# The blocks beyond an expert's slots: from a branch after every expert to one late place, and 96 slots for the largest expert

## The chip, the cores and the metric

One core of one Trainium2 chip runs the whole program in one launch. The metric is the device time of one execution in microseconds; of several executions the median is given. The kernel is fp32 throughout the part that the change touches. A row of the profile names an instruction by its line in kernel.py, its engine and the tiles that it writes and reads: PE is TensorE (PEld its weight loads), DVE is VectorE, ACT is ScalarE, POOL is GpSimd, SP is SyncE, which here only issues transfers. PEq, SPq and so on are the sequencers of those engines.

## What is computed

One layer of an encoder block on 256 tokens of width 1024: a layer norm, a gated attention mixer, a second layer norm, and then a mixture of 32 experts, of which each token takes its 4 best. The change touches the experts alone. Per expert the reference does, on the tokens that chose it,

```
hb = xb @ w_exp_in[e] + b_exp_in[e]          # 1024 -> 2048
g  = min(hb[:, :1024], 7);  u = clip(hb[:, 1024:], -7, 7)
y  = (g * sigmoid(1.702 * g) * (u + 1)) @ w_exp_out[e] + b_exp_out[e]   # 1024 -> 1024
```

and each token's four results are summed with its softmax weights. A last layer norm of `alpha * h + f` gives the output. How many tokens an expert gets is known only when the program runs; the 32 counts sum to 1024.

## The kernel before

**Places and slots.** All 32 experts are worked through, one after another, in 32 places (`for pos in range(NE)`, L1237). Places 0 and 1 hold experts 0 and 1 (`N_FIXED = 2`), since their numbers are known before the counts are. The other 30 are sorted by their counts while place 0 runs (`arrange`, L998 to L1031): the largest of them comes to place 3, the next ones to 5, 7 and so on to 29, the smaller ones to the even places 2, 4 ... 30, the smallest to 31. Odd places (and 0) have 64 slots (`CAP`), even places and place 31 have 32 (`HALF_CAP`); `width(pos)` at L934 says so. A slot holds one token. The table `meta` holds the expert at each place; SP reads it into a register (L950) to form the address of the weights.

**One place.** In order: `gemm1` (L1102) multiplies the gathered tokens by the first weights, in 8 steps over k; `act` (L1138) is the SwiGLU on DVE and ACT; `gather_rows` (L1061) picks the tokens of the next place by a matmul with a one-hot matrix; `scatter` (L1179) adds the results of the place before to the accumulators `acc`; `scatter_matrix`, `act_T` and `gather_T` are transposes through PE with a copy out by DVE or ACT; `gemm2` (L1160) multiplies by the second weights.

**Weights.** The weights of an expert are 12 MiB and come in six pieces of 2 MiB: four for `gemm1` (`load_in`, L958; piece i serves steps k = 2i and 2i + 1) and two for `gemm2` (`load_out`, L967). All are issued by SP in order. The pieces go through ten buffers in turn (`order`, L924), so piece number n lands in the buffer of piece n - 10: the `gemm2` pieces of place p take the buffers of the first two `gemm1` pieces of place p - 1, and the `gemm1` pieces of place p + 1 take those of the other two and of the `gemm2` pieces of place p - 1. SP can issue a transfer only when the last reader of its buffer is done.

**Blocks beyond the slots.** An expert may have more tokens than its place has slots. After `gemm2` of every place (for place 31 before its `gemm1`), `extras(pos, w1, w2)` at L1205 opens a branch for PE, ACT and DVE (`BRANCHING`, L1203). Its condition comes from `cnt` (places 0 and 1) or from `n_over`, the number of experts with more than 32 or 64 tokens (counted at L909 to L914, read into registers at L1273). Inside, under nested branches, stand blocks of 32 further slots (`extra`, L1186), each a whole gather, `gemm1`, `act`, `gemm2` and `scatter`. These blocks read the place's own weights, so those buffers are free only when the branch is past, taken or not. PE, ACT, DVE and POOL run in the order written (`in_order`, L832), SP too (`on_sp`, L1233).

**The end.** After place 31 come the last `scatter` (L1285), the layer norm and four stores (L1300).

Of the kernel before, what the change touches and what calls it, by code (L numbers as in the profile page):

```python
# [32 lines left out]
N_FIXED = 2  # L33
REL = 128
# [9 lines left out]
def kernel(  # L44
# [6 lines left out]
):  # L51

# [666 lines left out]
    cnt = const.tile([1, N_FIXED], I32, name="cnt")  # L719
# [16 lines left out]
    meta = mid.tile([1, NE + 2], I32, name="meta")  # L736
# [167 lines left out]
    V.tensor_copy(cnt, pc[0:1, 0:N_FIXED])  # L904
# [4 lines left out]
    over = keys[0:1, 2:4, :]  # L909
    for i in range(2):  # L910
        V.tensor_scalar(over[:, i, :], pc[0:1, :], float(HALF_CAP << i), None, op0=ALU.is_gt)
    n_over_f = mid.tile([1, 2], F32, name="n_over_f")
    V.tensor_reduce(n_over_f, over[:, :, N_FIXED:], axis=AX.X, op=ALU.add)
    V.tensor_copy(meta[:, NE:], n_over_f)  # L914
# [21 lines left out]

    def nth(pos):
# [5 lines left out]
    e_of = {}  # L943

    def expert(pos):

        if pos < N_FIXED:
            return pos
        if pos not in e_of:
            e_of[pos] = nc.values_load(meta[0:1, pos:pos + 1], engines=[ET.SP], min_val=0, max_val=NE - 1,  # L950
                                       skip_runtime_bounds_check_because="a place in a permutation of the experts")
        return e_of[pos]

    def of_expert(w, pos):
        e = expert(pos)
        return w[0, e] if pos < N_FIXED else w[0, bass.ds(e, 1)].rearrange("o r c -> (o r) c")

    def load_in(pos):  # L958
        w1 = []
        src = of_expert(w_exp_in, pos).rearrange("(i p k) f -> i p k f", p=P, k=2)  # L960
# [6 lines left out]
    def load_out(pos):  # L967
        w2 = []
        src = of_expert(w_exp_out, pos).rearrange("(i q p k) c -> i p q k c", q=2, p=P, k=2)
# [7 lines left out]
        return w2  # L977

# [19 lines left out]
    def arrange(step):  # L998
# [9 lines left out]
        if step == 1:  # L1008
# [8 lines left out]
            V.tensor_copy(cnt_pl, po[0:1, 2, :])  # L1017
        if step == 2:
# [28 lines left out]
    def onehots(pos, base, w, rk):  # L1047

        oh = mid.tile([P, NT, w], F32, name=f"oh{pos}_{base}", tag="t7" if base else "t6")
# [33 lines left out]
    def gather_T(pos, base, w, xr):  # L1083
# [6 lines left out]
        xe = (mid if base else keep).tile([P, KC, w], F32, name=f"xe{pos}_{base}", tag="t7" if base else "t1")  # L1090
# [47 lines left out]
    def act(pos, base, gu):  # L1138
        c = gu[0].shape[-1]
        both = keep.tile([P, 2, c], F32, name=f"a{pos}_{base}", tag="f1")  # L1140
        g, u = both[:, 0, :], both[:, 1, :]
        sg = keep.tile([P, c], F32, name=f"sg{pos}_{base}", tag="t2")
# [7 lines left out]
    def act_T(pos, base, w, a):  # L1150
# [5 lines left out]
        aT = (mid if base else keep).tile([P, m, P], F32, name=f"aTe{pos}_{base}", tag="t7" if base else "t3")  # L1156
# [29 lines left out]
    def extra(pos, base, w1, w2):  # L1186

        own = keep.tile([P, D], F32, name=f"own{pos}_{base}", tag="f2")
        y = own[:, 0:512]
        og = own[:, 512:768].rearrange("p (t s) -> p t s", t=NT)  # L1190
        st = own[:, 768:1024].rearrange("p (t s) -> p t s", t=NT)
        w = HALF_CAP
        rk = shifted(pos, base)
        xe = gather_T(pos, base, w, gather_rows(pos, base, w, onehots(pos, base, w, rk)))
        gated(pos, w, rk, og)
        gu = gemm1(pos, base, w, xe, w1)
        a = act(pos, base, gu)
        scatter_matrix(pos, base, og, st)
        py = gemm2(pos, base, w, act_T(pos, base, w, a), w2)
        A.copy(y, py)  # L1200
        scatter(st, y)

    BRANCHING = [ET.PE, ET.Activation, ET.DVE]  # L1203

    def extras(pos, w1, w2):  # L1205

        if pos < N_FIXED:
            most = S
            n_e = nc.values_load(cnt[0:1, pos:pos + 1], engines=BRANCHING, min_val=0, max_val=S)
            any_more = n_e > width(pos)  # L1210
        else:
            most = min(S, 4 * S // nth(pos))
            any_more = n_over[width(pos)] > nth(pos) - 1
        bases = range(width(pos), most, HALF_CAP)
        if not bases:
            return
        with tc.If(any_more, preferred_fallthrough_block=False):
            if pos >= N_FIXED and len(bases) > 1:
                n_e = nc.values_load(cnt_pl[0:1, pos:pos + 1], engines=BRANCHING, min_val=0, max_val=S)
            with ExitStack() as nest:  # L1220
                for base in bases:
                    if base > bases[0]:
                        nest.enter_context(tc.If(n_e > base, preferred_fallthrough_block=False))
                    extra(pos, base, w1, w2)

    n_over = {}
# [10 lines left out]
    for pos in range(NE):  # L1237
        more = pos + 1 < NE
        w = width(pos)
        w1, w2 = load_in(pos), load_out(pos)  # L1240
        if pos:
            results(y_of[:, (pos - 1) % 2], py)
        if not more:
            extras(pos, w1, w2)
# [14 lines left out]
        a = act(pos, 0, gu)  # L1259
        xr = gather_rows(pos + 1, 0, width(pos + 1), oh) if more else None  # L1260
# [7 lines left out]
        if more:  # L1268
            xe = gather_T(pos + 1, 0, width(pos + 1), xr)
        py = gemm2(pos, 0, w, aT, w2)  # L1270
        if pos == N_FIXED - 1:
            for i in range(2):
# [72 lines left out]
```

## Time and profile before

| what | us |
|---|---|
| median of 3 runs (1193.38 to 1194.40) | 1193.41 |
| the profiled execution, its own time | 1197.39 |
| its span, from the first to the last instruction | 1195.7 |
| PE busy | 967.5 (81%) |
| DVE / ACT / POOL busy | 284.4 / 192.1 / 55.3 |
| moved by DMA | 439.37 MB, 367 GB/s over the span |

The page cuts the span into 40 slices of 29.9 us. A digit is the busy share of an engine in that slice in tenths; the row GB/s gives what the 16 DMA engines moved in it. The experts start at about 216 us, in slice 7 (counted from 0).

### The profile page before, as it was taken

What the parts mean: (1) busy time and instruction counts of PE and PEld (TensorE: products, weight loads), DVE (VectorE), ACT (ScalarE), POOL (GpSimd) and SP (SyncE); (2) the same over time, 40 slices, a digit from 0 to 9 for tenths busy, and PEclk for the clock granted to TensorE, in tenths of its full rate; (3) what the DMA queues carried; (4) which work ended last, traced back from release to release, by engine and by line L of the source; (5) the groups of instructions that cost most, each with busy time, mean ns of one, the idle gap of its engine ahead of it and who ended that gap; (6) DMA issues with size and microseconds to landing.
All of it is one profiled execution on the core that took longest, in us unless ns stands there. A gap on an engine that the chain in (4) does not pass through costs nothing. (4 is left out here: it accounts for less than half of the span.)

```text
span 1195.7 us, 14309 instructions
## 1 busy us (share of the span) xinstructions
PE 967.5 (81%) x5767; PEld 433.4 (36%) x5767; DVE 284.4 (24%) x636; ACT 192.1 (16%) x413; POOL 55.3 (5%) x77
## 2 busy tenths in 40 slices
PE   9999999988778787868797877787767778777764
PEld 7989998322222222222222222222222222222211
DVE  6677577311111111111111111111111111111113
ACT  4366653100000000000000000000000000000011
POOL 3231201000000000000100000000000000000001
PEclk9999999999898998989898989898988989999978
DMA  8943568279939999999999999999999999999993
GB/s 287 374 142 135 207 271 346 77 314 400 425 148 425 424 424 423 424 423 424 416 424 423 424 424 423 425 423 425 423 425 423 414 424 424 425 423 426 423 423 144
DMA packets 52175, 439.37 MB, mean 367 GB/s; under 512 B 5006, under 2 KB 5102, under 8 KB 19538
## 3 DMA queue, kind: packets, MB, share of 16 engines
q1 hardware_dynamic: 50786, 434.29, 87.7%
q0 software_dynamic: 1120, 3.05, 0.8%
q8 instruction: 91, 1.49, 0.5%
q14 instruction: 34, 0.28, 0.1%
q10 hardware_dynamic: 144, 0.26, 0.1%
HBM read 436.14 MB, written 1.45 MB: 366 GB/s over the span
## 5 line engine op out<-in xcount | busy, mean ns | idle before, releaser
L1116 PE MATMUL gu<-w,xe 128*64 128x512 f32 x1024 | 245.9, 630 | 45.7 <-DMA w<-in_w_exp_in_dram 39.4
L1170 PE MATMUL py<-w,aTe 128*32 128x512 f32 (+1 forms) x1056 | 180.1, 607 | 13.5 <-DMA w<-in_w_exp_out_dram 11.0
L1119 PE MATMUL gu<-w,xe 128*32 128x512 f32 x1088 | 157.3, 712 | 29.3 <-DMA w<-in_w_exp_in_dram 22.6
L1116 PEld LDWEIGHTS gu<-w,xe 128*64 128x64 f32 x1024 | 76.1, 144 | 206.2 <-issue 156.6
L1143 DVE TENSOR_SCALAR a<-gu 128x256 f32<-128x256 f32 (+1 forms) x33 | 18.3, 554 | 540.0 <-PE gu L1116 279.3
L1144 ACT ACTIVATE sg<-a 128x256 f32<-128x256 f32 (+1 forms) x33 | 17.2, 520 | 580.9 <-DVE a L1143 580.9
L1170 PEld LDWEIGHTS py<-w,aTe 128*32 128x32 f32 (+1 forms) x1056 | 50.8, 124 | 117.7 <-issue 89.9
L1119 PEld LDWEIGHTS gu<-w,xe 128*32 128x32 f32 x1088 | 37.4, 127 | 133.5 <-issue 93.9
L1119 PE MATMUL gu<-be,sel_pl 96*32 96x512 bf16 x68 | 9.6, 556 | 83.1 <-issue 81.1
L165 PE MATMUL pT<-hT_hi,w 128*128 128x256 f32 x256 | 73.5, 287 | 0.0
L166 PE MATMUL pT<-hT_lo,w 128*128 128x256 f32 x256 | 72.1, 282 | 0.0
L167 PE MATMUL pT<-hT_hi,w 128*128 128x256 f32 x256 | 71.7, 280 | 0.0
L1177 DVE COPY y<-py 128x256 f32<-128x256 f32 x32 | 13.6, 424 | 222.0 <-ACT y L1176 213.3
L1184 PE MATMUL acc<-y,st 64*128 64x512 f32 x248 | 61.6, 615 | 0.0
L160 DVE TENSOR_TENSOR w<-win,w 128x512 fp32r<-128x512 f32 (+1 forms) x65 | 49.6, 785 | 35.3 <-ACT w L159 35.3
L159 ACT CAST w<-win 128x512 fp32r<-128x512 f32 (+1 forms) x74 | 46.2, 655 | 36.5 <-PE pT L166 23.3
L165 PEld LDWEIGHTS pT<-hT_hi,w 128*128 128x128 f32 x256 | 48.1, 188 | 1.9 <-issue 1.3
L167 PEld LDWEIGHTS pT<-hT_hi,w 128*128 128x128 f32 x256 | 48.4, 189 | 0.0
L166 PEld LDWEIGHTS pT<-hT_lo,w 128*128 128x128 f32 x256 | 48.2, 188 | 0.0
L1067 PE MATMUL px<-h,oh 128*32 128x256 f32 (+1 forms) x392 | 47.2, 452 | 0.0
L1176 ACT COPY y<-py 128x256 f32<-128x256 f32 x32 | 11.9, 372 | 165.9 <-PE py L1170 165.3
L1119 PEld LDWEIGHTS <-sel_pl 96*32 96x32 bf16 x68 | 1.9, 99 | 98.1 <-issue 98.0
(303 smaller groups left out, 850.2 us busy)
## 6 DMA issues: line engine op xcount, KB each, us to landing
w<-in_w_exp_in_dram SPq DMA_DIRECT2D x128, 2048.0 KB, 33.2
w<-in_w_exp_out_dram SPq DMA_DIRECT2D x63, 2048.0 KB, 25.7
win<-in_w_in_dram SPq DMA_DIRECT2D x9, 2048.0 KB, 17.7
wo<-in_w_out_dram SPq DMA_DIRECT2D x2, 2048.0 KB, 7.7
win<-in_w_in_dram SPq DMA_DIRECT2D x2, 1024.0 KB
wba<-in_w_branch_a_dram SPq DMA_DIRECT2D x1, 2048.0 KB
wbb<-in_w_branch_b_dram SPq DMA_DIRECT2D x1, 2048.0 KB
w<-in_w_exp_out_dram SPq DMA_DIRECT2D x2, 1024.0 KB, 24.0
```

The lines of the kernel that those rows point to most:

```text
L159: A.copy(hi, part)
L160: (eng[k // step % len(eng)] if isinstance(eng, tuple) else eng).tensor_tensor(lo, part, hi, op=ALU.subtract)
L165: T.matmul(dst, a[0], b[0], start=first, stop=False)
L166: T.matmul(dst, a[0], b[1], start=False, stop=False)
L167: return T.matmul(dst, a[1], b[0], start=False, stop=last)
L1067: T.matmul(px[i * w:(i + 1) * w, :], oh[:, t, :], h1[:, t, i * n:(i + 1) * n], start=(t == 0), stop=(t == NT - 1))
L1116: T.matmul(gu[i][q * w:(q + 1) * w, :], lhsT, rows[:, i, q * c:(q + 1) * c], start=first, stop=last)
L1119: T.matmul(both[q * w:(q + 1) * w], lhsT, rows[:, :, q * c:(q + 1) * c], start=first, stop=last)
L1143: V.tensor_scalar(g, gu[0], SW_LIMIT, None, op0=ALU.min)
L1144: A.activation(sg, g, AF.Sigmoid, scale=SW_ALPHA)
L1170: T.matmul(py[r:r + w, :], lhsT, w2[i][:, q, j, n * 512:(n + 1) * 512], start=(i == 0 and (m == 0 or w < CAP and m < 2)), stop=(i == 1 and ...
L1184: T.matmul(acc[t][n], st[r, t, :], y[r, :], start=False, stop=False)
```

## The change

`extras` and its branch after every place go, and with them `cnt`, `n_over` and the DVE instructions that filled them. The largest sorted expert, at place 3 (`SECOND`), gets 64 + 32 = 96 slots: its further block of 32 is cut into steps (`Further`) that are written into the straight program of places 2 and 3, and uses the weights while they are there. For every other place blocks beyond the slots stand in one late place, `beyond()`, called after `gemm2` of place 29 (`pos + 3 == NE`), under one branch whose condition is the number of places whose count is over `room`; each block there loads its expert's weights again, and SP is now among the branching engines. Nothing else of the places changes. The core of the diff:

```diff
+SECOND = 3
-    meta = mid.tile([1, NE + 2], I32, name="meta")
+    meta = mid.tile([1, NE + 1], I32, name="meta")
+    room = mid.tile([1, NE + 1], F32, name="room")
+    G.iota(room[:, 0:NE]..., pattern=[[0, NE // 2], [CAP - HALF_CAP, 2]], base=HALF_CAP, ...)
+    G.memset(room[:, 0:1], float(CAP))
+    G.memset(room[:, SECOND:SECOND + 1], float(CAP + HALF_CAP))
+    G.memset(room[:, NE - 1:NE], float(HALF_CAP))
...
-    V.tensor_copy(cnt, pc[0:1, 0:N_FIXED])
-    for i in range(2):
-        V.tensor_scalar(over[:, i, :], pc[0:1, :], float(HALF_CAP << i), None, op0=ALU.is_gt)
-    V.tensor_reduce(n_over_f, over[:, :, N_FIXED:], axis=AX.X, op=ALU.add)
-    V.tensor_copy(meta[:, NE:], n_over_f)
...                                       # arrange, step 1, behind cnt_pl
+            V.tensor_tensor(keys[0:1, 2, :], po[0:1, 2, :], room[:, 0:NE], op=ALU.is_gt)
+            V.tensor_reduce(room[:, NE:], keys[0:1, 2, :], axis=AX.X, op=ALU.add)
+            V.tensor_copy(meta[:, NE:], room[:, NE:])
...
-    def extra(pos, base, w1, w2):
...
-    BRANCHING = [ET.PE, ET.Activation, ET.DVE]
-    def extras(pos, w1, w2):
...
+    class Further:
+        def gather(self):
+            rk = shifted(*self.at)
+            oh = onehots(*self.at, HALF_CAP, rk)
+            gated(self.at[0], HALF_CAP, rk, self.og)
+            self.xr = gather_rows(*self.at, HALF_CAP, oh)
+        def turn(self):
+            gather_T(*self.at, HALF_CAP, self.xr, self.xe)
+        def first(self, w1):
+            self.a = act(*self.at, gemm1(*self.at, HALF_CAP, self.xe, w1), self.both, self.sg)
+        def second(self, w2):
+            scatter_matrix(*self.at, self.og, self.st)
+            py = gemm2(*self.at, HALF_CAP, act_T(*self.at, HALF_CAP, self.a, self.aT), w2)
+            A.copy(self.y, py)
+        def add(self):
+            scatter(self.st, self.y)
+
+    BRANCHING = [ET.PE, ET.Activation, ET.DVE, ET.SP]
+
+    def beyond():
+        n = nc.values_load(meta[0:1, NE:NE + 1], engines=BRANCHING, min_val=0, max_val=NE)
+        with tc.If(n > 0, preferred_fallthrough_block=False):
+            for pos in range(NE):
+                most = S if pos < N_FIXED else min(S, 4 * S // nth(pos))
+                bases = range(room_of(pos), most, HALF_CAP)
+                if not bases:
+                    continue
+                n_e = nc.values_load(cnt_pl[0:1, pos:pos + 1], engines=BRANCHING, min_val=0, max_val=S)
+                with ExitStack() as nest:
+                    for base in bases:
+                        nest.enter_context(tc.If(n_e > base, preferred_fallthrough_block=False))
+                        if base == bases[0]:
+                            w1, w2 = load(pos)
+                        block = Further(pos, base)
+                        block.gather(); block.turn(); block.first(w1); block.second(w2); block.add()
...                                       # in the loop over the places
         gu = gemm1(pos, 0, w, xe, w1, before)
         a = act(pos, 0, gu)
+        if pos == SECOND:
+            block.first(w1)
...
         if more:
             xe = gather_T(pos + 1, 0, width(pos + 1), xr)
+        if pos + 1 == SECOND:
+            block = Further(SECOND, CAP)
+            block.gather()
         py = gemm2(pos, 0, w, aT, w2)
-        if more:
-            extras(pos, w1, w2)
+        if pos + 1 == SECOND:
+            block.turn()
+        if pos == SECOND:
+            block.second(w2)
+            block.add()
+        if pos + 3 == NE:
+            beyond()
```

## Rows read from the trace of the kernel before

**Rows 1.** The page: the span, and of the span in 40 slices the rows of DMA (busy share in tenths, GB/s).
```profile
span 1195.7 us, 14309 instructions
...
DMA  8943568279939999999999999999999999999993
GB/s 287 374 142 135 207 271 346 77 314 400 425 148 425 424 424 423 424 423 424 416 424 423 424 424 423 425 423 425 423 425 423 414 424 424 425 423 426 423 423 144
```

**Rows 2.** The waits of SP's own queue: the waiting line, what it waited for, us in total, times, the longest.
```profile
SPq L975 <- PEq L1217: 591.1, 30, 42.3
...
SPq L975 <- PEq L1220: 49.2, 1, 49.2
```

**Rows 3.** Stretches around the early experts: the stretch in us, its length, busy us of each engine (instructions), then the granted clock, the DMA share and GB/s.
```profile
216.00:246.00 30.00, 27.50 (x140) 10.13 (x140) 5.54 (x18) 4.82 (x9) 0.00 (x0) 1.00 0.01 2
246.00:246.50 0.50, 0.00 (x0) 0.00 (x0) 0.50 (x4) 0.00 (x0) 0.00 (x0) 1.00 1.14 164
247.00:276.00 29.00, 27.05 (x132) 9.41 (x132) 3.19 (x5) 1.92 (x4) 0.00 (x0) 0.94 1.01 422
276.00:279.00 3.00, 0.37 (x2) 0.00 (x0) 1.26 (x5) 0.37 (x1) 0.00 (x0) 1.00 0.62 180
338.00:356.00 18.00, 14.39 (x104) 4.16 (x96) 3.21 (x10) 1.75 (x4) 0.00 (x0) 0.91 0.03 11
356.00:356.50 0.50, 0.00 (x0) 0.00 (x0) 0.00 (x0) 0.00 (x0) 0.00 (x0) 1.00 0.00 0
356.50:357.00 0.50, 0.00 (x0) 0.00 (x0) 0.00 (x0) 0.00 (x0) 0.00 (x0) 1.00 1.56 246
```

**Rows 4.** The timeline of SP: start us, us, queue, line, transfer, count.
```profile
245.16 0.89 SPq L975 DMA_DIRECT2D w<-in_w_exp_out_dram  x2
247.34 2.52 SPq L963 DMA_DIRECT2D w<-in_w_exp_in_dram  x4
...
355.57 1.01 SPq L975 DMA_DIRECT2D w<-in_w_exp_out_dram  x2
```

**Rows 5.** The instructions of the first DVE step of `act`, one per block (count, duration min/median/max, first and last start, forms).
```profile
L1143 DVE TENSOR_SCALAR a<-gu x33: 423/426/692, 233.6 to 1172.0; 128x256 f32<-128x256 f32 x17, 128x512 f32<-128x512 f32 x16
```

**Rows 6.** The timeline of DVE and PE at place 0: the last of the counting, `gemm1` in its four parts, the table `meta`, `gemm2`.
```profile
213.51 0.16 DVE L914 CAST meta<-n_over_f 1x2 int32<-1x2 f32 x1
...
216.21 5.37 PE L1116 MATMUL gu<-w,xe 128*64 128x512 f32 x24 [0.24 <-ACT xe L1091]
...
221.76 0.18 DVE L1011 CAST meta<-order_ps 1x32 int32<-1x32 f32 x1 [4.58 <-PE order_ps L1010]
...
222.69 3.65 PE L1116 MATMUL gu<-w,xe 128*64 128x512 f32 x16
...
226.82 3.65 PE L1116 MATMUL gu<-w,xe 128*64 128x512 f32 x16
...
231.41 1.94 PE L1116 MATMUL gu<-w,xe 128*64 128x512 f32 x8
...
237.94 7.09 PE L1170 MATMUL py<-w,aTe 128*64 128x512 f32 x32
```

**Rows 7.** The timeline of PE at places 1 to 3: the first matmul of each place with the idle time before it, `gemm2` of place 2, and of the further block of place 3 its gather, its `gemm1` and its `scatter`.
```profile
248.78 0.62 PE L1116 MATMUL gu<-be,sel_be 96*64 96x512 bf16 x4 [3.75 <-issue]
...
280.60 0.62 PE L1119 MATMUL gu<-be,sel_pl 96*32 96x512 bf16 x4 [4.23 <-issue]
...
296.10 3.64 PE L1170 MATMUL py<-w,aTe 128*32 128x512 f32 x32
306.56 1.06 PE L1116 MATMUL gu<-be,sel_pl 96*64 96x512 bf16 x4 [6.82 <-issue]
...
334.48 1.07 PE L1067 MATMUL px<-h,oh 128*32 128x256 f32 x16
...
337.11 7.07 PE L1119 MATMUL gu<-w,xe 128*32 128x512 f32 x64 [0.18 <-ACT xe L1091]
...
353.45 1.99 PE L1184 MATMUL acc<-own 64*128 64x512 f32 x8 [0.70 <-ACTq L1220]
```

**Rows 8.** The timeline of PE and SP at places 29 and 30; what stands in brackets is the idle time before and what ended it.
```profile
1117.55 7.09 PE L1170 MATMUL py<-w,aTe 128*64 128x512 f32 x32
...
1124.77 0.97 SPq L975 DMA_DIRECT2D w<-in_w_exp_out_dram  x2
...
1125.28 0.40 PE L1119 MATMUL gu<-be,sel_pl 96*32 96x512 bf16 x4 [0.65 <-PEq L1217]
...
1129.18 1.92 PE L1119 MATMUL gu<-w,xe 128*32 128x512 f32 x16 [1.77 <-DMA w<-in_w_exp_in_dram]
1134.09 3.28 PE L1119 MATMUL gu<-w,xe 128*32 128x512 f32 x16 [2.98 <-DMA w<-in_w_exp_in_dram]
```

**Rows 9.** A stretch at the end, in the form of rows 3.
```profile
1169.00:1180.00 11.00, 7.44 (x52) 2.24 (x52) 2.03 (x5) 0.79 (x2) 0.00 (x0) 1.00 0.46 189
```

**Rows 10.** The last matmul that waits for weights, in the timeline of PE, and of the page's DMA queues the one that brings instructions (packets, MB, share of 16 engines).
```profile
1180.02 1.06 PE L1170 MATMUL py<-w,aTe 128*32 128x512 f32 x8 [1.43 <-DMA w<-in_w_exp_out_dram]
...
q8 instruction: 91, 1.49, 0.5%
```

More of the change, by code (lines that the diff above doesn't have):

```diff
@@ L935, in width, with room_of @@
         return CAP if pos < N_FIXED or (pos % 2 and pos < NE - 1) else HALF_CAP
+    def room_of(pos):
+        return width(pos) + (HALF_CAP if pos == SECOND else 0)
     def nth(pos):
@@ L948, in expert, with of_expert, load_in @@
             return pos
[L949 to L958, printed above, removed]
+        return nc.values_load(meta[0:1, pos:pos + 1], engines=[ET.SP], min_val=0, max_val=NE - 1,
+                              skip_runtime_bounds_check_because="a place in a permutation of the experts")
+    def of_expert(w, e):
+        return w[0, e] if isinstance(e, int) else w[0, bass.ds(e, 1)].rearrange("o r c -> (o r) c")
+    def load_in(pos, e):
         w1 = []
-        src = of_expert(w_exp_in, pos).rearrange("(i p k) f -> i p k f", p=P, k=2)
+        src = of_expert(w_exp_in, e).rearrange("(i p k) f -> i p k f", p=P, k=2)
         for i in range(4):
@@ L977, in load_out, with load @@
         return w2
+    def load(pos):
+        e = expert(pos)
+        return load_in(pos, e), load_out(pos, e)
     gb2 = const.tile([3 * NE, P], BF16, name="gb2")
@@ L1136, in gemm1, with act @@
         return gu
-    def act(pos, base, gu):
+    def act(pos, base, gu, both=None, sg=None):
         c = gu[0].shape[-1]
-        both = keep.tile([P, 2, c], F32, name=f"a{pos}_{base}", tag="f1")
+        if both is None:
+            both = keep.tile([P, 2, c], F32, name=f"a{pos}_{base}", tag="f1")
+            sg = keep.tile([P, c], F32, name=f"sg{pos}_{base}", tag="t2")
         g, u = both[:, 0, :], both[:, 1, :]
-        sg = keep.tile([P, c], F32, name=f"sg{pos}_{base}", tag="t2")
         V.tensor_scalar(g, gu[0], SW_LIMIT, None, op0=ALU.min)
@@ L1184, in scatter @@
                 T.matmul(acc[t][n], st[r, t, :], y[r, :], start=False, stop=False)
-    def extra(pos, base, w1, w2):
[L1188 to L1201, printed above, removed]
@@ L1203, with __init__ @@
-    BRANCHING = [ET.PE, ET.Activation, ET.DVE]
-    def extras(pos, w1, w2):
[L1207 to L1218, printed above, removed]
+    class Further:
+        def __init__(self, pos, base):
+            self.at = pos, base
+            own = keep.tile([P, D], F32, name=f"own{pos}_{base}", tag="f2")
+            self.both = own[:, 0:512].rearrange("p (i c) -> p i c", i=2)
+            self.y = own[:, 0:512]
+            self.og = own[:, 512:768].rearrange("p (t s) -> p t s", t=NT)
+            self.st = own[:, 768:1024].rearrange("p (t s) -> p t s", t=NT)
+            more = mid.tile([P, 512], F32, name=f"more{pos}_{base}", tag="t7")
+            self.xe = more[:, 0:256].rearrange("p (k s) -> p k s", k=KC)
+            self.aT = more[:, 0:256].rearrange("p (j s) -> p j s", j=2)
+            self.sg = more[:, 256:512]
+        def gather(self):
[13 more added lines that the diff above has]
+            scatter(self.st, self.y)
@@ L1259 @@
         a = act(pos, 0, gu)
+        if pos == SECOND:
+            block.first(w1)
         xr = gather_rows(pos + 1, 0, width(pos + 1), oh) if more else None
@@ L1269 @@
             xe = gather_T(pos + 1, 0, width(pos + 1), xr)
+        if pos + 1 == SECOND:
+            block = Further(SECOND, CAP)
+            block.gather()
         py = gemm2(pos, 0, w, aT, w2)
-        if pos == N_FIXED - 1:
-            for i in range(2):
-                n_over[HALF_CAP << i] = nc.values_load(meta[0:1, NE + i:NE + i + 1], engines=BRANCHING, min_val=0,
-                                                       max_val=NE - N_FIXED)
-        if more:
-            extras(pos, w1, w2)
+        if pos + 1 == SECOND:
+            block.turn()
+        if pos == SECOND:
+            block.second(w2)
+            block.add()
+        if pos + 3 == NE:
+            beyond()
     y, st = y_of[:, (NE - 1) % 2], st_of[:, (NE - 1) % 2]
```

31 lines of the change are left out of this document (13 added, 18 removed).

## The prediction

> **What bounds the kernel now.** I read the page's slices first: from slice 12 on, DMA moves some 424 GB/s without a break, almost to the end, while slices 7 to 9 and 11 fall to 77, 314, 400 and 148 [rows 1]. So the experts are bound by the stream of weights. A piece of 2 MiB (2.097 MB) takes 4.95 us at 424 GB/s, six pieces, a place, 29.7 us, and where PE waits for pieces they come 4.91 us apart [rows 8]. In such a stretch a faster PE is worth nothing; only time in which the transfers stand still can be won.
>
> Next, the waits of SP, which issues them: 591.1 us in 30 waits for PE's sequencer at L1217, the branch of `extras`, the longest 42.3, and one of 49.2 at the nested branch [rows 2]. Most of it is covered by transfers already issued. The stretches show where it isn't [rows 3]: 216 to 246 us (share 0.01, so 29.7 us idle), 276 to 279 (0.62, 1.1 idle) and 338 to 356.5 (0.03, 18.0 idle). Sum: **48.8 us without weights**. The first ends with SP's issue at 245.16 [rows 4], just after `gemm2` of place 0 (237.94 + 7.09 = 245.03 [rows 6]): the next piece needs a buffer whose reader was done long before, but which the branch holds. The last is the further block: PE runs it alone from 334.48 to 355.44 [rows 7], and SP issues at 355.57 [rows 4].
>
> Did another branch run a block? `act` has 33 instances, 17 narrow ones for 16 narrow places [rows 5]: one further block in all, the one at place 3. The largest sorted expert has thus 65 to 96 tokens, and no other place is over its slots.
>
> **The change, term by term.** *Branches out of places 0 to 3.* Buffers of `gemm1` pieces now fall free as `gemm1` walks through k. 24 instructions take 5.37 us [rows 6], 8 per k, so k = 0 and 1 are done at 216.21 + 3.58 = 219.8. From issue to moving data the rows show about 1.1 us (245.16 to 246.0 or later, 355.57 to 356.5 or later [rows 3, 4]), so transfers resume at 220.9 instead of 246: 4.9 us idle after 216. Three more buffers come free by 233.4, sooner than four pieces take (220.9 + 19.8 = 240.7); the fifth waits for half of `gemm2`, 237.94 + 3.55 + 1.1 = 242.6: 1.9 us idle. The expert of place 2 stands in `meta` at 221.94 [rows 6], before its first piece can go.
>
> *The 96 slots in place 3.* The block's work is the same, but now inside the stream, so I ask whether PE falls behind by more than ten buffers. Place 1 can begin at 245.0 rather than 248.78 (3.75 us of idle after the skipped branch [rows 7] go) and takes 0.62 + 14.6 (the four parts of `gemm1` [rows 6]) + 4.6 + 7.09, to 272. Place 2 took 280.60 to 299.74 [rows 7]; with 2 us for the block's gather and turn it ends at 293. Place 3: 0.62 + 14.6 + 7.5 (the block's `gemm1` of 7.07 with its bias) + 4.6 + 7.09 = 34.4, to 327.5; the rest of the block is 21 us less its gather and `gemm1`, 11.3, and lets go of its first `gemm2` buffer some 6 us before its end, at 332.8. The queue, from 220.9 with 1.9 idle, has by 331.7 moved 22 pieces; the 23rd is the one that takes that buffer. So it stands still for about 2 us; a PE slower by 6 us, or quicker, gives 0 to 8. Idle left: 4.9 + 1.9 + 2 = 8.8, won: 48.8 - 8.8 = **40.0 us** (34 to 44).
>
> *The other branches* are hidden now behind transfers and stay so: nothing. What they may cost is instruction traffic: PE stands 3.75, 4.23 and 6.82 us after skipped branches with no releaser [rows 7], only 0.65 after a short skip [rows 8], and instruction packets are 91 with 1.49 MB [rows 10]. If half of these 1.49 MB goes, that is 1.8 us of DMA evenly spread; at the end, though, the engines are not even: from 1169 to 1180 the share is 0.46 while PE waits until 1180.02 for the last piece [rows 9, 10], so some run up to 10 us behind, and a packet that hits these costs more. Bounds 0 and 8; I take **3**, nearer to the even spread.
>
> *The late place.* SP now branches too, and the pieces for place 30 take buffers that blocks in the branch would use. On the skipped side SP waits until all transfers issued have landed, and its next pieces wait for PE past `gemm2` of place 29. In the kernel before these pieces were issued a place earlier. So the stream runs dry once. The last piece of place 29 lands two pieces before the wait that ended at 1129.18, at 1119.4; `gemm2` ends at 1124.64, and SP issued at 1124.77 [rows 8]; with 1.1 us data moves at 1125.9: 6.5 us idle. SP's own jump: if it stands as PE did, 3.75 to 6.82 us from 1119.4, and then reads the expert (246.05 to 247.34, 1.3 us [rows 4]), it issues between 1124.5 and 1127.5: up to 9.2 idle, and up to 12 if the first piece after a restart is slow in landing. PE stood after each of the three long skips, so I take **8.5**, nearer to the case in which SP stands too. PE's own jump is hidden: the first piece lands some 6 us later. The Trainium skill (Runtime: NRT & Kernel Launch, Instruction fetch mechanics) says that a taken branch whose target is outside the window already fetched must wait for its page to be loaded, and calls that one reason why run-time control flow is dear. PE's idle time after long skips, 3.75 to 6.82 us, agrees; by that rule SP stands as well and the term is about 9, without it 6.5.
>
> *At nothing:* five DVE instructions leave before 213.7 [rows 6], but `gemm1` of place 0 waits for ACT's copy; three of their size come after 222.8, where DVE idles; `room` is five POOL instructions in an earlier stage. If uncovered, under 1 us. The end behind the last piece is unchanged.
>
> **Sum:** 40.0 + 3 - 8.5 = 34.5. The profiled execution took 1197.39 us, so 1162.9; the median of the runs is 4.0 lower, which gives **1159 us**. A measurement here can tell about 0.2%, 2.4 us.
>
> **The rivals.** *PE becomes the limit at place 3* (0.10): if the longer place starves the ring, the 18 us stay: 1159 + 16 = 1175. For it: place 3 takes 34.4 + 11.3 = 46 us against 29.7 of weights. Against: ten buffers hold 49.5 us of transfers.
>
> *The first gap stays* (0.04): SP issues in order, so one piece that is still held keeps back all behind it. If the first is let go only after `gemm2`, 23 us of the 40 are lost: 1182. Against: in the program nothing but `gemm1` reads it now.
>
> *The late place is dear* (0.10): the jump on SP, DVE, ACT and PE and the empty queue cost 20 us and not 8.5: 1170. Against: the longest stand after a skip is 6.82 us. It is what the rule of the Trainium skill on taken branches would come to if several engines stood one behind another.
>
> *The late place is free* (0.08): SP gets past and the pieces of place 30 are on their way before `gemm2` ends: 1150. Against: their buffers are those of the branch.
>
> *Slower: the late branch is taken* (0.03). One place over its room is enough. Then six pieces are loaded again (29.7 us), the block's rest of some 10 us follows their landing, and the queue restarts once more (8.5): about 48, to 1207, over 1193.41. Against it: one further block only, at the place that now has 96 slots [rows 5].
>
> **How the numbers follow.** Forecast 0.65: best 44 + 8 - 6.5 = 45.5 off the median, 1148; worst 34 + 0 - 12 = 22, 1171. This range takes in the dear late place and most of the free one; what is left out, the first gap, PE as the limit and the taken branch, is 0.17. So 1147 to 1171. Faster by over 0.2%: all but the taken branch, 0.97, less 0.02 for what I don't see; that 0.02 is shared by the other two, so 0.95, within 0.2% 0.01, slower 0.04.
>
> **What would show it.** In the profile after: DMA idle after 216 us for about 5 us and not 30; no hole near 340; SP's waits for the branch gone but one; in each place PE's idle time with no releaser gone; PE waiting for pieces from about place 8 on; one hole of 7 to 12 us after `gemm2` of place 29, some 40 us earlier than now. Wrong is this if the hole near 340 is still there (PE as the limit), if the first hole is over 20 us, or if the late hole is over 15 us.

## The result and the profile after

The changed kernel takes **1152.07 us** (median of 4 runs, 1148.51 to 1154.31), the kernel before took 1193.91 us beside it (4 runs): ratio 0.9637, 95% interval 0.9600 to 0.9675, by this ratio 43 us less, the interval 39 to 48 (the medians differ by 42). The forecast was 1159. The profiled execution took 1154.31 us with a span of 1152.6; line numbers below are those of the changed kernel, in which `gemm1` is L1123 (64 slots) and L1126 (32), `gemm2` L1179, `load_in` L962, `load_out` L974, `scatter` L1193 and the branch of `beyond()` L1235.

The page's span, the stream in 40 slices (now of 28.8 us) and the queue of instructions answer to [rows 1, 10]:

```profile
span 1152.6 us, 14117 instructions
...
GB/s 285 384 164 81 203 267 363 311 390 426 426 412 427 429 426 426 427 427 428 427 426 425 427 428 426 426 426 426 428 425 428 426 426 428 426 427 353 288 426 199
...
q8 instruction: 47, 0.77, 0.3%
```

The deep slices 7 and 11 are gone (77 and 148 GB/s before). The steady part runs at 426 to 428, not 423 to 425. A new dent, 353 and 288, stands near the end; the packets of instructions fell from 91 to 47.

SP's waits, in the form of [rows 2]:

```profile
SPq L962 <- PE py L1179: 98.3, 33, 14.6
SPq L1235 <- SPq L1235: 32.0, 2, 27.0
SPq L962 <- PEq L1235: 8.4, 1, 8.4
```

The 591.1 us behind PE's branch after each place, and the 49.2 behind the nested one, are gone. What SP waits for on PE is now the last reader of a buffer, and once, for 8.4 us, PE's new branch. PE in turn waits 147.3 us for the pieces of `gemm1` (90.6 + 56.7; before, these waits were 62.0), as it must when the stream is the bound. Its stands with no releaser, 25 with 116.2 us in the matmuls of `gemm1` before, are one of 5.8. These stands in the kernel before, then the rows of the one after:

```profile
PE gu L1119 <- issue: 87.6, 17, 7.1
PE gu L1116 <- issue: 28.6, 8, 6.8
```

```profile
PE gu L1126 <- DMA w<-in_w_exp_in_dram: 90.6, 42, 3.0
PE gu L1123 <- DMA w<-in_w_exp_in_dram: 56.7, 39, 2.7
PE gu L1126 <- issue: 5.8, 1, 5.8
```

**The early places.** The stretches in the form of [rows 3], then SP and PE in those of [rows 4, 6, 7]:

```profile
204.00:212.00 8.00, 7.06 (x43) 4.23 (x40) 7.45 (x33) 3.32 (x5) 3.64 (x4) 1.00 0.94 391
214.50:220.00 5.50, 5.49 (x26) 1.69 (x26) 0.24 (x2) 0.00 (x0) 0.00 (x0) 1.00 0.32 69
236.00:260.00 24.00, 24.00 (x126) 8.16 (x125) 4.00 (x9) 2.13 (x5) 0.00 (x0) 1.00 0.95 383
300.00:340.00 40.00, 38.09 (x272) 12.50 (x268) 8.24 (x20) 4.57 (x10) 3.95 (x9) 1.00 1.01 418
```

```profile
218.17 5.15 SPq L974 DMA_DIRECT2D w<-in_w_exp_out_dram  x2
```

```profile
214.48 5.37 PE L1123 MATMUL gu<-w,xe 128*64 128x512 f32 x24 [0.24 <-ACT xe L1098]
236.22 7.09 PE L1179 MATMUL py<-w,aTe 128*64 128x512 f32 x32
243.13 0.60 PE L1123 MATMUL gu<-be,sel_be 96*64 96x512 bf16 x4
287.27 0.62 PE L1123 MATMUL gu<-be,sel_pl 96*64 96x512 bf16 x4
301.79 7.05 PE L1126 MATMUL gu<-w,more 128*32 128x512 f32 x64
```

SP issues at 218.17 where it issued at 245.16. Between the start of `gemm1` of place 0 and 260 the stream stands 0.68 x 5.5 + 0.05 x 24 = 4.9 us, and from 300 to 340 not at all. Place 1 starts right at the end of `gemm2` of place 0 (236.22 + 7.09 = 243.3), with no stand ahead of it, and the `gemm1` of the further block (301.79) follows place 3's own without a gap.

**The late place.** Stretches around it and, last, the 11 us before the last piece (in the form of [rows 9]); then PE and SP in the form of [rows 8]:

```profile
1057.00:1066.00 9.00, 8.96 (x47) 3.16 (x43) 3.19 (x5) 1.01 (x3) 0.00 (x0) 0.81 0.51 208
1066.00:1078.00 12.00, 7.53 (x34) 2.46 (x34) 1.23 (x5) 1.28 (x3) 0.00 (x0) 1.00 0.29 89
1125.94:1136.94 11.00, 8.53 (x52) 2.46 (x53) 2.03 (x5) 0.79 (x2) 0.00 (x0) 0.84 0.85 348
```

```profile
1066.64 7.09 PE L1179 MATMUL py<-w,aTe 128*64 128x512 f32 x32 [0.19 <-ACT aTe L1166]
1079.56 0.62 PE L1126 MATMUL gu<-be,sel_pl 96*32 96x512 bf16 x4 [5.83 <-issue]
1082.83 2.79 PE L1126 MATMUL gu<-w,xe 128*32 128x512 f32 x12 [2.65 <-DMA w<-in_w_exp_in_dram]
```

```profile
1073.86 2.22 SPq L962 DMA_DIRECT2D w<-in_w_exp_in_dram  x4
```

The shares from 1057 to 1078 leave 0.49 x 9 + 0.71 x 12 = 4.4 + 8.5 = 12.9 us idle. SP issues the pieces of place 30 at 1073.86, 0.13 us after `gemm2` of place 29 (1066.64 + 7.09). PE then stands 5.83 us with nothing that it waits for, and after that another 2.65 us for its piece: the stand is hidden.

**The stream in between**, from 400 to 1040 us, in the kernel before and in the one after:

```profile
400.00:1040.00 640.00, 495.89 (x2756) 159.67 (x2752) 82.21 (x216) 49.84 (x108) 6.48 (x17) 0.91 1.01 423
```

```profile
400.00:1040.00 640.00, 505.85 (x2792) 157.81 (x2792) 84.92 (x220) 50.92 (x110) 0.00 (x0) 0.93 1.01 427
```

The share is 1.01 in both, and yet 423 GB/s became 427.

**The sum, from these rows** (span against span, 1195.7 - 1152.6 = 43.1):

| where | us |
|---|---|
| idle time of places 0 to 3: 48.8 [rows 3], now 4.9 | +43.9 |
| rate between the holes: 146 pieces of 2.097 MB, 306.2 MB, at 423 and at 427 GB/s (723.9 and 717.1 us) | +6.8 |
| late hole | -12.9 |
| the 11 us before the last piece: idle 5.9 (share 0.46 [rows 9]), now 1.6 (share 0.85) | +4.3 |
| `gemm1` of place 0 starts at 214.48, not at 216.21 [rows 6]: ahead of the change | +1.7 |
| together | +43.8 |

The 146 pieces lie between the 33rd of the experts and the 179th, behind the early holes and ahead of the late one. The rates are whole numbers in the rows; half a unit is 0.8 us. The start of place 0 is no part of the change: of the kernels below, e0, the changed kernel again, starts it at 212.59 and e5, which has the change too, at 216.50, while e7, the kernel before without its block, starts it at 214.08.

### The profile page after: what moved, and what is told of

Same layout as the page of the kernel before. It is cut to its first block, busy times and chain, and to the rows that moved or that the text cites. A ratio compares the mean times of both kernels' runs of the same rounds, so it can differ in the third digit from the quotient of the medians.

```text
span 1152.6 us, 14117 instructions
## 1 busy us (share of the span) xinstructions
PE 959.3 (83%) x5767; PEld 426.8 (37%) x5767; DVE 284.9 (25%) x634; ACT 192.1 (17%) x413; POOL 55.6 (5%) x81
## 5 line engine op out<-in xcount | busy, mean ns | idle before, releaser
L1123 PE MATMUL gu<-w,xe 128*64 128x512 f32 x1024 | 240.3, 618 | 59.6 <-DMA w<-in_w_exp_in_dram 56.7
L1126 PE MATMUL gu<-w,xe 128*32 128x512 f32 x1024 | 153.7, 733 | 90.6 <-DMA w<-in_w_exp_in_dram 90.6
L1179 PE MATMUL py<-w,aTe 128*64 128x512 f32 (+1 forms) x1024 | 173.9, 598 | 10.1 <-DMA w<-in_w_exp_out_dram 6.8
L1123 PEld LDWEIGHTS gu<-w,xe 128*64 128x64 f32 x1024 | 75.2, 141 | 215.1 <-issue 148.4
L1151 DVE TENSOR_SCALAR a<-gu 128x512 f32<-128x512 f32 (+1 forms) x32 | 17.9, 558 | 486.6 <-PE gu L1123 255.7
L1152 ACT ACTIVATE sg<-a 128x512 f32<-128x512 f32 (+1 forms) x32 | 16.7, 523 | 539.2 <-DVE a L1151 539.2
L1126 PEld LDWEIGHTS gu<-w,xe 128*32 128x32 f32 x1024 | 31.4, 121 | 193.3 <-DMA w<-in_w_exp_in_dram 130.7
L1179 PEld LDWEIGHTS py<-w,aTe 128*64 128x64 f32 (+1 forms) x1024 | 49.7, 123 | 111.1 <-issue 87.0
L1193 PE MATMUL acc<-y,st 64*128 64x512 f32 x248 | 61.6, 615 | 0.0
L1073 PE MATMUL px<-h,oh 128*32 128x256 f32 (+1 forms) x392 | 50.0, 467 | 0.7 <-ACT xe L1098 0.7
L117 POOL TENSOR_TENSOR ln_r<-ln_ve,nhalf 128x1 f32<-128x1 f32 x6 | 3.4, 559 | 861.2 <-DVE ln_ve L115 860.3
L1193 PEld LDWEIGHTS acc<-y,st 64*128 64x128 f32 x248 | 21.3, 186 | 34.1 <-issue 20.2
## 6 DMA issues: line engine op xcount, KB each, us to landing
w<-in_w_exp_out_dram SPq DMA_DIRECT2D x63, 2048.0 KB, 39.2
win<-in_w_in_dram SPq DMA_DIRECT2D x9, 2048.0 KB, 17.7
```

The lines of the kernel that those rows point to most:

```text
L1073: T.matmul(px[i * w:(i + 1) * w, :], oh[:, t, :], h1[:, t, i * n:(i + 1) * n], start=(t == 0), stop=(t == NT - 1))
L1123: T.matmul(gu[i][q * w:(q + 1) * w, :], lhsT, rows[:, i, q * c:(q + 1) * c], start=first, stop=last)
L1126: T.matmul(both[q * w:(q + 1) * w], lhsT, rows[:, :, q * c:(q + 1) * c], start=first, stop=last)
L1151: V.tensor_scalar(g, gu[0], SW_LIMIT, None, op0=ALU.min)
L1152: A.activation(sg, g, AF.Sigmoid, scale=SW_ALPHA)
L1179: T.matmul(py[r:r + w, :], lhsT, w2[i][:, q, j, n * 512:(n + 1) * 512], start=(i == 0 and (m == 0 or w < CAP and m < 2)), stop=(i == 1 and ...
```

## The experiments

The theory after the result: the time is the stream of weights plus the time in which it stands; a branch costs where it holds a buffer that the stream needs next, and otherwise little, because PE's stands are hidden in its waits for weights. The rivals: the branches cost by themselves (their jumps, their instruction packets), wherever they stand; or the further block, not the branch, is what cost.

Kernels of one table group ran side by side with the kernel before (medians 1194.98, 1196.66, 1194.54 and 1195.83 us); each ratio is to that.

| kernel | us | ratio, 95% interval |
|---|---|---|
| e0: the changed kernel again | 1148.71 | 0.9623, 0.9601 to 0.9646 |
| e1: without the late place | 1141.49 | 0.9554, 0.9538 to 0.9570 |
| e2: late place after place 28 | 1147.63 | 0.9603, 0.9584 to 0.9622 |
| e3: late place after place 31 | 1144.60 | 0.9588, 0.9567 to 0.9608 |
| | | |
| e4: block of place 3 in one piece | 1157.63 | 0.9684, 0.9660 to 0.9708 |
| e5: 25 skipped bodies of 300 matmuls | 1192.35 | 0.9968, 0.9950 to 0.9986 |
| e6: branch back at place 0 alone | 1173.78 | 0.9812, 0.9789 to 0.9836 |
| e7: kernel before, without its block | 1178.56 | 0.9857, 0.9826 to 0.9888 |
| | | |
| e8: 25 skipped bodies of 2 matmuls | 1151.75 | 0.9645, 0.9628 to 0.9663 |
| e9: 8 skipped bodies of 300 | 1154.57 | 0.9674, 0.9654 to 0.9693 |
| e10: e5 without the late place | 1159.98 | 0.9718, 0.9700 to 0.9736 |
| | | |
| e11: 25 skipped bodies of 40 | 1154.04 | 0.9653, 0.9632 to 0.9675 |

### e0 and e1: what the late place costs

> The changed kernel itself, once more, beside the three variants of its late place. Every theory: the median of its four runs, 1152 us, within their spread of 1148.5 to 1154.3.

> The changed kernel without its late place: the branch and all that stands in it left out (for these inputs nothing in it runs). Theory: the branch makes the stream of weights run dry once, and the profile of the changed kernel puts 11.1 us on it (a landing 15.99 us after the one before instead of 4.93). So 1152 - 11 = 1141 us, and no hole in the stream after place 29. Rival (the stream would have been late anyway, the hole hides other lag): 1149 to 1152.

```diff
-        if pos + 3 == NE:
-            beyond()
```

e1 leaves out blocks beyond the room of a place; with these inputs there are none. It takes 1141.49 us against 1148.71 of e0: the late place costs **7.2 us**. The time is the 1141 of the theory, the cost is not its 11, since e0 was 3.3 us below the 1152 that this was taken from. The rival (the stream would have been late anyway: 1149 to 1152) fails. The 7.2 us are also less than the stream stands in e0's late hole, and the end shows why. The hole of e0 and the 11 us before its last piece, then those 11 us in e1:

```profile
1052.00:1072.00 20.00, 15.01 (x80) 5.41 (x80) 4.42 (x10) 2.29 (x5) 0.00 (x0) 0.95 0.52 198
1119.46:1130.46 11.00, 8.88 (x52) 2.65 (x52) 2.03 (x5) 0.79 (x2) 0.00 (x0) 0.84 0.84 345
```

```profile
1112.20:1123.20 11.00, 8.88 (x53) 2.58 (x53) 2.03 (x5) 0.79 (x2) 0.00 (x0) 0.84 0.57 238
```

The hole is 0.48 x 20 = 9.6 us. Without it the 16 DMA engines end unevenly (share 0.57, so 4.7 us are lost while the slowest still works), with it they have met again shortly before (0.84, 1.8 us). Some 3 us of the 9.6 come back, and 6.6 are left. That the engines drift apart can be read from the trace, in which each piece reports 16 landings: for the last pieces of e1 the first and the last of the 16 lie 8.5 us apart, for those of e0, behind its hole, 1.8 to 2.0.

### e2 and e3: another place for the late place

> The late place moved up by one, from behind place 29 (64 slots) to behind place 28 (32 slots). Theory: the hole is what PE still has to do after the last weights of the place have landed, plus some 4 us of restart. Behind 64 slots PE ended 6.9 us after that landing; behind 32 slots half a second matmul stage, 1.9 us. So the hole shrinks from 11 to about 6 us: 1147 us. Rival (the hole is made by SP, which jumps over a long piece of program): it stays at 11, 1152.

```diff
-        if pos + 3 == NE:
+        if pos + 4 == NE:
             beyond()
```

1147.63 us, 1.1 below e0, and the intervals overlap: the time alone decides nothing. The hole did get shorter:

```profile
1024.00:1040.00 16.00, 12.00 (x72) 3.75 (x72) 3.27 (x10) 2.33 (x5) 0.00 (x0) 0.90 0.58 218
```

0.42 x 16 = 6.7 us against 9.6; `gemm2` of the narrow place takes 3.64 us and not 7.09. That only 1 of these 2.9 us shows in the time comes from the stage before the experts, at least in the two profiled executions: `gemm1` of place 0 starts at 214.44 in e2 and at 212.59 in e0, and from there to the last piece (1129.45 and 1130.46) e2 needs 2.9 us less.

> The late place moved behind the last matmul of place 31, where no weights are to come (its tiles in other buffers). Theory: no hole in the stream, but the jump now lies in the chain of the end: PE stands 4 to 6 us before the last scatter, where it stood 5.83 us behind the branch in the changed kernel. So 1152 - 11 + 5 = 1146 us. Rival (the hole is the price of the jump itself, wherever it is): 1152.

```diff
-        if pos + 3 == NE:
+        if pos + 1 == NE:
             beyond()
```

(and three tiles of the block come from buffers that are free at the end.) 1144.60 us, 4.1 below e0 and 3.1 above e1. There is no piece left to hold back, so no hole; what stays is PE's stand, now in the open, between the last `gemm2` and the last `scatter`:

```profile
1126.54 3.79 PE L1319 MATMUL acc<-y,st 64*128 64x512 f32 x8 [4.33 <-issue]
```

Of the versions that still take any counts this one has the lowest time; its interval meets those of e0 and e2.

### e4: the block's steps inside the place, or behind it

> The changed kernel with the further block of place 3 in one piece behind the second matmul stage of place 3 (where the branch had it), not in steps within places 2 and 3; no branch. Theory (buffers): the first weights of place 3 are then held until the block's first matmul stage some 14 us later, the 29th piece can be issued only at about 318 us and not at 304, and the stream has a hole of 4 to 11 us there: 1156 to 1163. Rival (what counts is that the branch is gone, the steps are of no use): 1152 to 1154.

```diff
-        if pos == SECOND:
-            block.first(w1)
...
-        if pos + 1 == SECOND:
-            block.gather()        # likewise turn(), before place 3
         py = gemm2(pos, 0, w, aT, w2)
         if pos == SECOND:
+            block.gather(); block.turn(); block.first(w1)
             block.second(w2)
             block.add()
```

1157.63 us, as expected by the theory. The stream and PE:

```profile
300.00:315.00 15.00, 14.05 (x98) 5.04 (x98) 1.47 (x7) 1.66 (x4) 0.00 (x0) 1.00 0.61 254
```

```profile
311.95 7.08 PE L1126 MATMUL gu<-w,more 128*32 128x512 f32 x64 [0.18 <-ACT more L1098]
```

The block's `gemm1`, the last reader of the place's first pieces, ends at 319.0 and not at 308.8, and the stream stands 0.39 x 15 = 5.9 us, where the changed kernel shows nothing from 300 to 340. That is about the difference of the ratios to e0 and e4, 0.0061, or 7 us. Ten buffers do not cover the block by themselves: its `gemm1` has to stand early here.

### e6 and e7: the two holes one by one

> The changed kernel with the branch of the kernel before put back behind place 0 alone: not taken, but its block reads the weights of place 0. Theory (held buffers): the first hole comes back, since the next piece is issued at 245 us and not at 218; the stream loses 20 to 24 us: 1172 to 1176. Rival (a branch costs the stand of PE behind it, 4 to 7 us): 1156 to 1159, or 1152 where weights hide it.

```diff
+        if pos == 0:
+            n_0 = nc.values_load(cnt_pl[0:1, 0:1], engines=[ET.PE, ET.Activation, ET.DVE], ...)
+            with tc.If(n_0 > CAP, preferred_fallthrough_block=False):
+                block = Further(0, CAP)
+                ...                        # gather, turn, first(w1), second(w2), add
```

1173.78 us: one branch that is not taken, whose body reads the weights of place 0, costs 0.019 of 1196.66, **23 us** over e0 (25 by the medians). The whole first hole is back:

```profile
SPq L974 <- PEq L1310: 40.4, 1, 40.4
```

```profile
216.00:246.00 30.00, 28.02 (x146) 10.36 (x144) 5.63 (x18) 4.67 (x8) 0.00 (x0) 1.00 0.05 10
```

```profile
244.34 0.62 PE L1123 MATMUL gu<-be,sel_be 96*64 96x512 bf16 x4 [0.67 <-PEq L1310]
```

0.95 x 30 = 28.5 us idle, and PE stood only 0.67 us at this jump. So the jump is not the price; the held buffer is. That 23 and not 28.5 - 4.9 us show in the time is within the intervals.

> The kernel before, with the branch of place 3 left out: its further block isn't computed (the 5 tokens beyond 64 slots of that expert are dropped). All other branches stay. Theory: the hole near 340 us goes, 18 us, the first hole of 30 stays: 1194 - 18 = 1176. Rival (the first hole only moves the wait; PE is the limit of the first places, and what the block takes is all that can be won): 1194 - 21 - 7 = 1166 or less.

```diff
-        if not bases:
+        if not bases or pos == 3:
             return
```

(in `extras`; it drops the tokens of place 3 beyond 64.) 1178.56 us against 1196.66 of the kernel before: **18.1 us** (17.1 by the ratio), the length of the last hole. From 338 to 350, where the stream stood, it runs:

```profile
338.00:350.00 12.00, 11.23 (x82) 3.65 (x76) 2.03 (x5) 1.96 (x4) 0.00 (x0) 1.00 1.02 426
```

### e5, e8 to e11: what a skipped branch costs when it holds nothing

> The changed kernel with a skipped branch for PE, ACT and DVE behind each of the places 4 to 28, over a body of 300 matmuls that reads no weights and never runs. Theory (instruction packets): the jumps bring back some 40 instruction packets of 16 KB but hold no buffer, and the stream is again about 0.075 us slower per piece, in all 6 to 10 us: 1158 to 1162. Rival (the stream is quicker because more transfers are issued ahead, not because of fewer packets): 1152. Second rival (the time was won by relieving PE of the jumps, 4 to 7 us for each of 25): 1200 or more.

```diff
+        if 3 < pos < 29:
+            ...                        # n_more is read once, for PE, ACT and DVE
+            with tc.If(n_more > 0, preferred_fallthrough_block=False):
+                ...                    # a tile pw
+                for _ in range(300):
+                    T.matmul(pw, ident, ident, start=True, stop=True)
+                ...                    # a tile spare
+                V.tensor_copy(spare, pw)
+                A.copy(spare, pw)
```

1192.35 us: 43.6 over e0 (41 by the ratios), and neither the theory (1158 to 1162) nor the rivals (1152, if the stream gained by more transfers issued ahead; 1200 or more, if PE was relieved of its jumps) had that. The trace:

```profile
PE gu L1126 <- issue: 91.3, 16, 6.9
PE gu L1123 <- issue: 86.1, 15, 6.7
PE gu L1126 <- DMA w<-in_w_exp_in_dram: 17.7, 8, 3.0
```

```profile
352.92 1.06 PE L1123 MATMUL gu<-be,sel_pl 96*64 96x512 bf16 x4 [6.24 <-issue]
```

```profile
1080.00:1113.00 33.00, 29.22 (x158) 9.96 (x152) 4.42 (x10) 2.29 (x5) 0.00 (x0) 0.95 0.03 13
1113.00:1118.00 5.00, 0.69 (x4) 0.00 (x0) 1.23 (x5) 0.37 (x1) 0.00 (x0) 0.87 0.67 206
```

PE stood 31 times with no releaser, 177.4 us together (the changed kernel: 5.8): after each of the 25 skips, 24 times 6.1 to 6.9 us and once 3.55, five times for 0.9 to 5.2 us in the `gemm1` that follows, and once at `beyond()`. Its waits for the pieces of `gemm1` shrank from 147.3 us to 17.7: PE had used up its slack, and was far behind when it reached the late place. There the stream stands until `gemm2` of place 29 is done, now from 1080 to 1115: 0.97 x 33 + 0.33 x 5 = 33.7 us instead of 12.9. PE's delay shows in full in the time: `gemm2` of place 29 ends 46.5 us later than in e0 (1113.70 against 1067.24), and the span is 46.8 us longer (1192.9 against 1146.1). The packets of instructions rose to 97.

New theory: a jump over a long body makes PE stand some 6 us; that is free while PE waits for weights for longer than that in each place, and beyond it it moves the end, most of all at a point where the stream waits for PE. Four kernels to test it:

> The skipped branches behind places 4 to 28 again, at the same places and under the same condition, but the body that is jumped over has 2 matmuls and not 300. Theory (the dear thing is a jump over a long body: in the run with long bodies PE stood 31 times, 5.7 us each, with no releaser): the stands shrink to some 0.7 us each, PE waits for pieces again, the instruction packets stay near 47 and not 97, and the time is that of the changed kernel, 1149 to 1154. Rival (any taken branch of three engines costs that much, however short): 1185 to 1195, with stands of over 5 us still there.

```diff
-                for _ in range(300):
+                for _ in range(2):
```

> The skipped branches behind places 4 to 28 with bodies of 40 matmuls, between the 2 matmuls that left no stand of PE (1151.75 us) and the 300 that left 31 stands of 5.7 us (1192.35 us). Theory (a stand is the loading of instructions at a target that is not there yet; it is there or it is not): a stand is either missing or 5 to 6 us long; with 40 matmuls and their 40 weight loads jumped over at least a third of the 25 skips still have their target at hand, so 0 to 16 stands, under 95 us in all, which PE's slack of some 145 us takes up: 1148 to 1157, instruction packets between 48 and 75. Rival (the stand grows with the number of instructions jumped over): 25 stands of some 0.8 us each. Rival (anything but a short body costs the whole stand): 25 stands, 1180 or more.

```diff
-                for _ in range(300):
+                for _ in range(40):
```

1151.75 and 1154.04 us, as expected. The matmul behind the skip of place 4, in e8 and in e11:

```profile
345.03 0.62 PE L1123 MATMUL gu<-be,sel_pl 96*64 96x512 bf16 x4 [0.47 <-PEq L1311]
```

```profile
345.26 0.62 PE L1123 MATMUL gu<-be,sel_pl 96*64 96x512 bf16 x4 [0.47 <-PEq L1311]
```

0.47 us in both, 6.24 in e5 at the same spot. Behind all 25 skips of e8 and of e11 the idle time is 0.43 to 0.63 us; the only stand of over 1 us left is that at `beyond()`. The stand does not grow in proportion to the instructions jumped over: 2 and 40 matmuls cost the same, in e6 a whole block of some 130 costs 0.67, 300 cost 6.1 to 6.9, and the branch after place 0 of the kernel before, over six such blocks, stood 3.75 [rows 7]. Where between 130 and 300 it begins was not tried. The Trainium skill (Runtime: NRT & Kernel Launch, Instruction fetch mechanics) says that a taken branch whose target lies outside the pages at hand must wait for a fetch; these runs agree, with no stand over up to some 130 matmuls and one over 300. That it is the fetch that PE waits for is not shown otherwise, though e5 has 50 packets of instructions more than the changed kernel.

> The long skipped bodies (300 matmuls) behind places 4 to 11 only, 8 of the 25. Theory (a stand of PE costs nothing until PE's slack is used up; in the run with 25 the 177 us of stands exceeded the some 146 us in which PE waits for pieces): 8 stands of 5.8 us make 46 us, which PE makes good in the places 12 to 29, and the late hole is as in the changed kernel; 16 instruction packets more cost about 1 us: 1149 to 1155. Rival (each skip takes 43.6 / 25 = 1.7 us out of the stream itself): 1149 + 14 = 1163, 1160 to 1166.

```diff
-        if 3 < pos < 29:
+        if 3 < pos < 12:
```

1154.57 us, as expected by the theory, although PE stands 58.6 us:

```profile
PE gu L1126 <- issue: 32.4, 6, 6.6
PE gu L1123 <- issue: 26.2, 5, 6.4
```

PE makes them good in places 12 to 29. The rival, each skip taking its 1.7 us out of the stream, would have given 1160 to 1166.

> The 25 long skips again, and the late place left out. Theory (with the skips PE is behind the stream, so that the late place, where the stream stands until PE is done, costs more than the 7.2 us that it costs without them: its hole was some 34 us long and not 12): against the run with skips and the late place the time falls by about 20, to 1165 to 1175; what stays over 1141.5, some 28, is the stream held by PE and PE's tail behind the last piece. Rival (the late place costs the same with a late PE): 1192 - 7 = 1185.

```diff
-        if pos + 3 == NE:
-            beyond()
```

1159.98 us, below both: the direction is the theory's, the size is not. With PE late the late place costs **32.4 us** (1192.35 - 1159.98; 30 by the ratios), not the 20 that I expected, against 7.2 with PE on time. PE works without a single wait for weights to the end, and its last `gemm2` ends at 1143.8. The `gemm2` of place 29 and the last one, in e10 and in e5:

```profile
1106.11 7.09 PE L1179 MATMUL py<-w,aTe 128*64 128x512 f32 x32 [0.19 <-ACT aTe L1166]
1140.14 3.64 PE L1179 MATMUL py<-w,aTe 128*32 128x512 f32 x32 [0.52 <-ACT aTe L1166]
```

```profile
1106.61 7.09 PE L1179 MATMUL py<-w,aTe 128*64 128x512 f32 x32 [0.19 <-ACT aTe L1166]
1177.24 1.06 PE L1179 MATMUL py<-w,aTe 128*32 128x512 f32 x8 [1.07 <-DMA w<-in_w_exp_out_dram]
```

Up to place 29 the two are alike. From the end of its `gemm2` to the end of the last one e10 needs 1143.8 - 1113.2 = 30.6 us and e5 1178.3 - 1113.7 = 64.6. This is what I had missed: without the late place the weights of the two last places are in the ring while PE is behind, so PE works them off at its own pace; with it the stream starts only when PE is done, and PE, behind no longer, has to wait for twelve pieces.

## Why the prediction was right, and where its sizes were off

**The bound.** Right: the stream ran at its rate before and after, and only time in which it stood was won.

**The holes, +40.0 (34 to 44).** Measured +43.9, the top of the range. The mechanism held at each step: SP issued at 218.17 (forecast 219.8), the second stop, before `gemm2` of place 0 frees its buffer, was 1.2 us (forecast 1.9). The step that failed is the queue at place 3, "so it stands still for about 2 us": from 300 to 340 the share is 1.01. Place 3 began at 287.27 and not at 293 (1.7 us of it the earlier start), so the buffer that the queue needs was free in time (`gemm2` of the block, its last reader, starts at 322.13; the forecast had that buffer free at 332.8). e4 shows how near the limit was: with the block's `gemm1` behind `gemm2` there is a hole of 5.9 us. By single changes e6 gives 23 us for the first hole and e7 18.1 for the last.

**The instruction packets, +3 (0 to 8).** Measured +6.8, as a higher rate at the same DMA share: inside the bounds, but more than twice the size, and the cause that I named carries only part of it. I stayed near the even spread, 1.8 us for half of 1.49 MB; with 44 packets and 0.72 MB fewer came almost four times that. At first sight the rate from 400 to 1040 goes with the number of packets: 45 to 48 in the whole run give 427 GB/s (after, e0, e1, e6, e8), 63 give 426 (e9, e11), 88 and 91 give 423 (e7 and before). The jumps are not it: e8 has 25 of them, 48 packets and 427. That packets cost something e9 shows within one run, with its skips up to 570 us and none behind; but the kernel before, last, is slower still in the first of these stretches:

```profile
400.00:600.00 200.00, 159.33 (x864) 53.23 (x858) 24.37 (x65) 14.28 (x32) 0.00 (x0) 0.89 1.01 425
600.00:1040.00 440.00, 351.72 (x1994) 110.02 (x1990) 61.42 (x159) 36.99 (x80) 0.00 (x0) 0.95 1.01 427
```

```profile
400.00:600.00 200.00, 154.96 (x868) 49.66 (x868) 24.93 (x66) 15.16 (x33) 4.27 (x11) 0.91 1.01 422
```

From 400 to 600 both have 18 packets in queue q8 (and 3 and 8 in q14, the only other queue of instructions), the changed kernel 7 (and 2); e5 and e10 have 19 and also run at 425. So packets go with some 1 to 2 of the 4 GB/s, not with all of them. Nor do transfers issued further ahead explain the rest: from issue to landing a piece of `gemm1` takes 32.4 us there in the kernel before and 39.2 in the changed one, but only 25.2 in e9. What makes the rest of the 6.8 us stays open.

**The late place, -8.5 (6.5 to 12).** Net -8.6 by the profiles (12.9 in the hole, 4.3 back at the end), 7.2 by e0 and e1: the size held, its make-up did not, so that the size is in part luck. I let SP wait for the last landing and then stand at its own jump as PE does. SP was past both of its branches before `gemm2` of place 29 began (the row shows duration min/median/max in ns, then first and last start), was ready to issue at 1065.5 (1073.86 less its wait of 8.4 us for PE), and issued 0.13 us after that `gemm2`. The trace has the last landing of place 29 at 1066.70: SP had waited for the pieces before it alone.

```profile
L1235 SPq COMPARE_BRANCH  x2: 37/45/53, 1029.7 to 1062.2; - x2
```

What I had not foreseen is that the DMA engines run dry one after another from 1057 on and not together (4.4 us until 1066), and that this part is won back at the end, where they now finish together. PE's stand of 5.83 us was hidden, as forecast. The hole as a whole is 0.9 us over the 7 to 12 named ahead, and stands 50.9 us earlier (`gemm2` of place 29 at 1066.64, against 1117.55 [rows 8]), not some 40.

**The other branches at nothing.** Right in this kernel, with the cover named: PE's waits for weights. e5 and e10 show what comes when that cover is gone: the same late place costs 30 to 32 us.

**Outside the terms.** 1.7 us came from the stage before the experts. From 204 to 212 us the granted clock was 1.00 in this execution (first of the early rows above) and 0.57, so for most of it at the lower of its two levels, in that of the kernel before:

```profile
204.00:212.00 8.00, 7.99 (x32) 5.26 (x31) 5.14 (x23) 3.00 (x4) 3.60 (x4) 0.57 0.97 410
```

It goes with the execution and not with the change: e5 has 0.58 there and starts place 0 at 216.50, e10 0.57 and 216.31, e7, without the change, 1.00 and 214.08.

**Together.** The profiled execution was to take 1162.9 us and took 1154.31, 8.6 less: 3.9 from the holes, 3.8 from the rate, 1.7 from the start, less 0.1 for the late place and 0.7 that the rows sum to too much. That of the kernel before was 4.0 above its median, this one 2.2, which takes 1.8 off the miss: 1152.07 against 1159. Of the rivals none happened: no hole near 320 to 340 (PE as the limit), none of over 20 us at 216, no branch taken; and e1 shows that the late place was neither free nor 20 us dear.

## What to carry to other kernels

A branch that is not taken still holds every buffer that its body reads: find the queue that waits for it, see whether the next transfer needs such a buffer, and cost the branch there, not by its jump. A jump over a long body costs its engine a stand (over 300 matmuls here 6 to 7 us), which is free as long as the sum of the stands in a stage is below the time in which that engine waits for data there, and sets the end beyond that. A point where the stream must wait for an engine costs that engine's delay (in e5 all of it), so it belongs where the engine is least behind, or after the last transfer.

## What had not been expected of the hardware

- The stand after a jump comes as a step: 0.43 to 0.63 us over 2 or 40 matmuls, 0.67 over some 130, 6.1 to 6.9 over 300 in 24 of 25 cases.
- The weight stream ran at 423 and not 427 GB/s, 0.9% less, at the same DMA share of 1.01, in the kernel with 91 instruction packets against that with 47; an even spread of the 0.72 MB between them over 1150 us would make 0.15%, and e9, in a stretch with as many packets, lost some 2 GB/s and not 4.
- The 16 DMA engines drift apart in a long stream: 5.9 us of the last 11 lost before, 4.7 in e1; the 16 landings of a piece lie 12.1 and 8.5 us apart there, 1.8 and 3.8 near 370. One break shortly before the end puts them together again (1.6 and 1.8 us lost; 2.0 us apart or less).
